# Reciprocal square roots on VectorE, residual steps scheduled earlier, three up-projection steps interlaced

## The chip, the core and the metric

The kernel runs on one core of one Trainium2 chip. The metric is the device time of one execution in microseconds. The core's engines run at the same time, each through its own queue in order: TensorE (PE in the profile, its weight loads PEld), VectorE (DVE), ScalarE (ACT), GpSimd (POOL) and SyncE (SP), which issues the weight loads.

## What is computed

A decoder trunk of four layers over one sequence of 256 tokens, 1024 wide, in float32. Each layer is a token mixer and a squared-ReLU MLP, each behind an RMS norm and added to the residual; the mixers are differential attention (layers 0 and 3), block-sparse MoBA (layer 1) and sliding-window attention with sinks (layer 2). A last RMS norm ends it.

```python
def rms_norm(x, g):
    y = x * rsqrt(mean(x * x, axis=-1, keepdims=True) + 1e-6)
    return y * g

def diff_attention(h, ...):                 # layers 0 and 3, 8 heads
    ...
    p = softmax(s)                          # two score maps for each head
    p = p[:, :, 0] - lam * p[:, :, 1]
    o = einsum('bhqk,bkhe->bqhe', p, v)
    o = rms_norm(o, sub_g) * (1.0 - lambda_init)
    return o.reshape(B, S, H * 128) @ w_out

def sqrelu_mlp(h, w_up, w_down):
    a = maximum(h @ w_up, 0)
    return (a * a) @ w_down

for i in range(4):
    h = h + mixer[i % 3](rms_norm(h, attn_norm_g[i]))
    h = h + sqrelu_mlp(rms_norm(h, mlp_norm_g[i]), w_up[i], w_down[i])
return rms_norm(h, final_norm_g)
```

So there are reciprocal square roots of three kinds: one for each layer's first norm, one for each head in the two differential layers, and one for the final norm. (The second norm of each layer goes through the squared ReLU: its factor is applied afterwards as a plain reciprocal of the mean square.)

## The kernel before

**Weights.** All weights come as pieces of 128 x 2048 float32 (1 MB). `fetch` issues the load of one piece on SyncE's queue into one of four `raw` buffers. `stage` splits it into a high part `whi` (ScalarE, line 80) and the remainder `wlo` (VectorE, line 81), in two halves of 1024 columns. `take` hands out a piece, having fetched five and staged two ahead. Activations are split in the same way, and each product is three matmuls: high by high, high by low, low by high. `mm3` (lines 267 to 269) writes three of 256 columns for the output projections; `block_step` (lines 605 and following) does it with two matmuls, one 512 columns wide over both halves of the activation (`hi`) and one 256 wide (`lo`).

**Layout.** The residual is kept transposed in four tiles `hT`, each with two of the eight 128-row blocks d. `into` (lines 615 to 628) adds a finished block of a projection to `hT` (VectorE, line 625) and calls `norm_part`, which makes that block's part of the next norm's input: `hg`, the residual times the gain, its high part on ScalarE (line 224) and its low part on VectorE (line 225). `norm_sum` gathers the squares.

**First norm of a layer.** The input projection `p_in` (line 292) runs on `hg` without the norm's factor. `norm_factor` sums the squares with a matmul (`p_sum`), makes `nx` (VectorE, line 247) and takes the root: `nr`, by `rsqrt` (lines 206 and 207). The first readers of `nr` apply it to the output of `p_in`: ScalarE in layers 0, 1 and 3 (`qk`, line 589), VectorE in layer 2 (`rest`, line 495, then rope, lines 300 to 305, then the transposes `p_qk`, line 461).

**Differential heads.** In layers 0 and 3 heads go in pairs, four pairs a layer. `diff_pair` multiplies by the values (`p_av`), sums squares on ScalarE (`junk`), makes `ss` (VectorE, line 399), the root `ry`, the scaled output `o` (VectorE, line 403, which reads the PSUM bank of `p_av`), its transposes `p_o` (line 408) and their split `oo`. New heads' queries and keys go through `p_qk`, `qhl`, `kpadh` (ScalarE, line 477) and `kpadl` (VectorE, line 478), the scores through `p_s` and the readings `ns` (line 332).

**Output projection.** `out_proj_all` (layers 0, 2, 3) holds all eight blocks in four PSUM banks (`p_d`) and goes through four pieces; `rest()` finishes the last heads within it. Only the fourth piece (g = 3) completes a block, and `into` follows for each of the eight. Layer 1 uses `out_proj`.

**MLP.** `up_proj` takes 16 pieces; each gives two blocks of 128 hidden rows in two banks (`p_up`), over eight input blocks k. For the first piece (g = 0) the steps are sorted by k, so that TensorE can begin when the first `hg` is there; then for k = 0 to 7 comes a step for b = 0 and one for b = 1. `down_proj` follows.

**Order.** The program is written as straight code; a scheduler places the instructions of each engine by priority, which by default is the order in the code, and by its own estimate of when the inputs are there. So one engine's queue is fixed when the program is built, and an edit can move instructions far from it. PSUM is used as two groups of four banks, "wk" (scores, transposes, `p_up`) and "acc" (`p_in`, `p_d`).

Of the kernel before, what the change touches and what calls it, by code (L numbers as in the profile page):

```python
# [11 lines left out]
F32 = mybir.dt.float32  # L12
F32R = mybir.dt.float32r
I32 = mybir.dt.int32
AF = mybir.ActivationFunctionType
OP = mybir.AluOpType
AX = mybir.AxisListType

P = 128
D = 1024  # L20
S = 256
NT = S // P
# [12 lines left out]
def f(ap):  # L35
    return ap.bitcast(F32)
# [3 lines left out]
def trunk(ctx: ExitStack, tc: tile.TileContext, xT, gains, lams, swa_row, fng, weights, out):  # L40
    nc = tc.nc
    V, A, G, T = nc.vector, nc.scalar, nc.gpsimd, nc.tensor

    cst = ctx.enter_context(tc.tile_pool(name="cst", bufs=1))
    tiny = ctx.enter_context(tc.tile_pool(name="tiny", bufs=2))
# [3 lines left out]
    def bank(tag, name):  # L49
        return ps.tile([P, 512], F32, tag=tag, name=name, bufs=4)  # L50
# [44 lines left out]
    def r3(n):  # L95
        return lambda t: t.rearrange("p (a b) -> p a b", a=n)
# [29 lines left out]
    invt = cst.tile([P, NT, 8], F32, name="invt")  # L126
    for j in range(8):
        G.memset(invt[:, :, j:j + 1], float(inv[j]))
    minus_half = cst.tile([P, 2 * NT], F32, name="minus_half")
    G.memset(minus_half, -0.5)  # L130
    make_identity(nc, ident)

# [70 lines left out]
            V.tensor_scalar(nlam[:, s:s + 1], nlam[:, s:s + 1], -lam_init[s], None, op0=OP.add)  # L203
            V.tensor_scalar(sg[:, s:s + 1], sg[:, s:s + 1], 1.0 - lam_init[s], None, op0=OP.mult)

    def rsqrt(y, x):
        G.tensor_tensor(y, x, minus_half[:, :x.shape[-1]], op=OP.pow)


    class Normed:  # L210
# [30 lines left out]
    def mean_square(n):  # L241

        p = bank("wk", "p_sum")
        for t in range(NT):
            T.matmul(p[:, P * t:P * t + P], n.acc[:, P * t:P * t + P], ones, start=True, stop=True)
        x = tiny.tile([P, NT], F32, tag="nx", name="nx", bufs=8)
        V.tensor_scalar(x, p[:, :S].rearrange("p (t m) -> p t m", m=P)[:, :, 0], 1.0 / D, EPS, op0=OP.mult, op1=OP.add)
        return x

    def norm_factor(n):  # L250

        x = mean_square(n)
        r = tiny.tile([P, NT], F32, tag="nr", name="nr")
        rsqrt(r, x)
        return r

    def mean_row(n):
# [96 lines left out]
    def times_v(o, et, v):  # L354

        T.matmul(o(0), et[:, 0:P], v(0), start=True, stop=True)
        T.matmul(o(1), et[:, P:2 * P], v(0), start=True, stop=False)
        T.matmul(o(1), et[:, 2 * P:3 * P], v(1), start=False, stop=True)
# [9 lines left out]
    def part(b, n=1):  # L368

        if b % 2 == 0:  # L370
            pair[:] = [room(14 + b // 2, [P, 2, 2, S], "oo", F32R)]
        return pair[0] if n == 2 else pair[0][:, b % 2]
# [17 lines left out]
    def diff_pair(slot, ets, v, el, b):  # L390

        p = bank("wk", "p_av")
        for c in range(2):
            times_v(lambda t, c=c: p[:, S * c + P * t:S * c + P * t + P], ets[c], v[c])
        ss = tiny.tile([P, 2 * NT], F32, tag="ss", name="ss")
        for t in range(2 * NT):
            junk = sb.tile([P, P], F32, tag="junk", name="junk", bufs=1)
            A.activation(junk, p[:, P * t:P * t + P], AF.Square, accum_out=ss[:, t:t + 1])
        V.scalar_tensor_tensor(ss, ss, 1.0 / P, el, op0=OP.mult, op1=OP.add)
        y = tiny.tile([P, 2 * NT], F32, tag="ry", name="ry")  # L400
        rsqrt(y, ss)
        o = sb.tile([P, 2 * NT, P], F32, tag="o", name="o")
        V.tensor_tensor(o, p.rearrange("p (t m) -> p t m", m=P), y[:, :, None].to_broadcast([P, 2 * NT, P]),
                        op=OP.mult)
        yield
        p = bank("wk", "p_o")
        for t in range(2 * NT):
            T.transpose(p[:, P * t:P * t + P], o[:, t, :], ident)
        both, gain = part(b, 2), sg[:, slot:slot + 1]
        A.activation(both[:, :, 0], r3(2)(p), AF.Copy, scale=gain)  # L410
        V.scalar_tensor_tensor(both[:, :, 1], r3(2)(p), gain, f(both[:, :, 0]), op0=OP.mult, op1=OP.subtract)
        yield [both[:, 0], both[:, 1]]
# [66 lines left out]

    def mixer_layer(i, n):  # L480
        mixer, slot = i % 3, i // 3
        r = norm_factor(n)
        parts = []
        kpad = new_keys()
        if mixer == 2:
# [6 lines left out]
            p = proj(n, (256, 1), True)  # L492
            kv = rest[:, 512:1024].rearrange("p (t c) -> p t c", t=NT)
            for t in range(NT):
                V.scalar_tensor_tensor(kv[:, t, :], p[t], r[:, t:t + 1], rest[:, :256],
                                       op0=OP.mult, op1=OP.add)
# [4 lines left out]
            for c in range(4):  # L501
                p = proj(n, (256, 1), False, first)
                qn = room(c % 2, [P, NT, 256], "qn")
                for t in range(NT):
                    for h in range(2):
                        s = slice(P * h, P * h + P)
                        o = qn[:, t, :].rearrange("p (b h e) -> p b h e", h=2, e=HD)[:, :, h, :]
# [19 lines left out]
        else:  # L527
# [40 lines left out]
            order = (0, 1, "v", 2, 3, "v") if mixer else (0, 1, "v", 2, "v", 3)  # L568
# [9 lines left out]
            for at, c in enumerate(order):  # L578
                p = proj(n, (512, 2), at == 0, [lambda do=do, x=x: do(x) for do, x in plan[2 * at]])
# [22 lines left out]

    def block_step(p, hi, lo, x, start, stop):
        T.matmul(r3(2)(p), hi, x, start=start, stop=False, skip_group_check=True)  # L606
        T.matmul(p[:, :S], lo, x[:, 0], start=False, stop=stop, skip_group_check=True)  # L607

    def joined(out, p):

        cross = sb.tile([P, S], F32, tag="cross", name="cross")
        A.activation(cross, p[:, S:], AF.Copy)  # L612
        V.tensor_tensor(out, p[:, :S], cross, op=OP.add)  # L613

    def into(n, d, p, row, whole=False):

        j, b = d // 2, d % 2
        h = hT[j][:, S * b:S * b + S]
        y = p
        if not whole:  # L620
            y = sb.tile([P, S], F32, tag="y", name="y")
            joined(y, p)
        if row is not None:
            V.tensor_tensor(y, y, row, op=OP.mult)
        V.tensor_tensor(h, y, h, op=OP.add)  # L625
        norm_part(n, d)
        if b:
            norm_sum(n, j)

    def out_proj_all(parts, n, rest):  # L630

        banks = [bank("acc", f"p_d{j}") for j in range(4)]
        for g in range(4):
            hi, lo = (r3(2)(x) for x in take())
            for d in range(8):
                if (g, d) == (2, 4):
                    rest()
                p = banks[d // 2][:, S * (d % 2):S * (d % 2) + S]
                w = slice(P * d, P * d + P)
                for a in range(2):  # L640
                    x = parts[2 * g + a]
                    mm3(p, hi[:, a, w], lo[:, a, w], x[:, 0], x[:, 1], g + a + d % 2 == 0, g + a == 4,
                        skip_group_check=True)
                if g == 3:
                    into(n, d, p, None, True)

    def out_proj(parts, n, rest):

# [16 lines left out]
    def up_proj(n, then):  # L665

        us = []
        for g in range(16):
            hi, lo = (r3(8)(x) for x in take())
            ps_up = [bank("wk", "p_up") for _ in range(2)]  # L670
            order = [(b, k) for b in range(2) for k in range(8)]
            for b, k in order if g else sorted(order, key=lambda x: x[1]):
                w = slice(P * b, P * b + P)
                block_step(ps_up[b], hi[:, k, w], lo[:, k, w], n.both[k // 2][:, k % 2], k == 0, k == 7)
            t = sb.tile([P, 512], F32, tag="relu", name="relu")
            for b in range(2):
                joined(t[:, S * b:S * b + S], ps_up[b])
            u = sb.tile([P, 512], F32, tag="u", name="u")
            V.scalar_tensor_tensor(u, t, 0.0, t, op0=OP.max, op1=OP.mult)  # L679
            both = room(g, [P, 2, 2, S], "uu", F32R)  # L680
            A.activation(both[:, :, 0], r3(2)(u), AF.Copy)  # L681
            V.tensor_tensor(both[:, :, 1], r3(2)(u), f(both[:, :, 0]), op=OP.subtract)  # L682
            us += [both[:, b] for b in range(2)]
            then(g)
        return us
# [10 lines left out]
    def down_out(us, res, factor):  # L696
# [3 lines left out]
        ss = cst.tile([P, 4, NT], F32, name="fss")  # L700
        x = cst.tile([P, 2, NT], F32, name="fx")
        r = cst.tile([P, NT], F32, name="fr")
# [10 lines left out]
        def finish(t, halves):  # L713

            o = slice(t, t + 1)
            y = r[:, o]
            V.scalar_tensor_tensor(x[:, 1, o], ss[:, halves, o], 1.0 / D, x[:, 0, o], op0=OP.mult, op1=OP.add)
            rsqrt(y, x[:, 1, o])
            rows = slice(P * t, P * t + P)
            A.activation(res[t][:, :512], res[t][:, :512], AF.Copy, scale=y)  # L720
            nc.scalar.dma_start(out[rows, :512], res[t][:, :512])
            for z in (slice(512, 768), slice(768, 1024)):
                V.scalar_tensor_tensor(res[t][:, z], res[t][:, z], y, grow[:, z], op0=OP.mult, op1=OP.mult)
                nc.sync.dma_start(out[rows, z], res[t][:, z])
# [7 lines left out]
        for c in range(2):  # L732
# [22 lines left out]
            if c == 0:  # L755
                last(1, ends)
                close(1, banks[1], 0, 0)
                for t in range(NT):
                    y = res[t][:, :512]
                    V.tensor_tensor(y, y, grow[:, :512], op=OP.mult)  # L760
                    sofar(t, [])
            else:
# [4 lines left out]
                for h in range(2):  # L767
                    p = bank("acc", "p_last")[:, :256]
# [8 lines left out]
    n = new_norm(gv[:, 0, 0, :])  # L777
# [5 lines left out]
    for i in range(DEPTH):  # L783
        parts, rest = mixer_layer(i, n)
        n = new_norm(gv[:, 1, i, :])
# [24 lines left out]
        if i + 1 < DEPTH:  # L810
            n = new_norm(gv[:, 0, i + 1, :])
# [81 lines left out]
```

## Time and profile before

| | |
|---|---|
| median of 3 runs | 1145.63 us (1145.61 to 1146.57) |
| the profiled execution, its own time | 1146.1 us |
| its span | 1144.3 us (1.8 us lie around it) |
| granted TensorE clock, mean | 0.998 |
| powers on GpSimd (line 207) | 14 in 14.5 us: ry 8, nr 4, fr 2 |
| tensor work: weights read | 196.52 MB, 173 GB/s over the span |

The profile is of one execution. A line of a group gives line, engine, operation, output and inputs, the count, then busy time and mean duration in ns of one instruction, then the idle time of the engine just before these and what ended it. The chain of waits is followed back from the last instruction; its columns are start, length and what ran. The timeline lists instructions by start and length. "POOL" is GpSimd, "DVE" VectorE, "ACT" ScalarE.

### The profile page before, as it was taken

How to read it: one execution, taken by the hardware profiler on the slowest of the kernel's cores; microseconds unless marked ns; L12 is line 12 of the kernel's file. 1: busy time of each engine (PE TensorE's matmuls, PEld its weight loads, DVE VectorE, ACT ScalarE, POOL GpSimd, SP SyncE). 2: the span in 40 equal slices, each digit the busy share in tenths (PEclk: the TensorE clock that was granted, in tenths of full speed). 3: DMA queues.
4: the chain of work that ended last, by engine and by line, in shares of the span. 5: the costliest groups of instructions: out<-in, count | busy, mean ns of one | idle time of the engine just before them, and what ended most of it. 6: DMA issues, size and time to landing. Idle time of an engine off the chain costs nothing.

```text
span 1144.3 us, 16938 instructions
## 1 busy us (share of the span) xinstructions
PE 1135.1 (99%) x6560; PEld 987.1 (86%) x6560; DVE 808.9 (71%) x1474; ACT 660.6 (58%) x1207; POOL 25.9 (2%) x54
## 2 busy tenths in 40 slices
PE   9999999999999999999999999999999999999997
PEld 7889888888888888888899898888888889888886
DVE  7867977656576698776568887775657677777453
ACT  7866655544476665654446866554447666665332
POOL 2000000000100000000010000000010000000000
PEclk9999999999999999999999999999999999999999
DMA  8543455555544355555563346555553434555551
GB/s 327 199 147 118 167 198 189 198 198 184 184 143 151 115 182 190 198 200 185 184 208 111 111 148 220 184 185 187 185 201 130 148 143 153 188 198 180 184 184 37
DMA packets 30608, 198.66 MB, mean 174 GB/s; under 512 B 3520, under 2 KB 5184, under 8 KB 7360
## 3 DMA queue, kind: packets, MB, share of 16 engines
q1 hardware_dynamic: 30240, 197.06, 49.6%
q8 instruction: 51, 0.84, 0.3%
q10 hardware_dynamic: 288, 0.52, 0.1%
q14 instruction: 29, 0.24, 0.1%
HBM read 196.52 MB, written 1.05 MB: 173 GB/s over the span
## 4 chain that ended last, share of the span: by engine, by line
PE 94%; DVE 2%; issue 1%; ACT 1%; DMA 0%; POOL 0%; SPq 0%; POOLq 0%; DVEq 0%; ACTq 0%
PE p_up L606 21%; PE p_in L292 18%; PE p_down L606 15%; PE p_up L607 11%; PE p_down L607 8%; PE p_last L269 2%; PE p_last L268 2%; PE p_last L267 2%; PE p_d L268 2%; PE p_d L269 2%; PE p_d L267 2%; PE p_t L350 1%; DVE wlo L81 1%; PE p_s L267 1%; PE p_s L268 1%; PE p_av L432 1%
## 5 line engine op out<-in xcount | busy, mean ns | idle before, releaser
L81 DVE TENSOR_TENSOR wlo<-raw,whi 128x1024 fp32r<-128x1024 f32 (+1 forms) x374 | 446.8, 1210 | 210.6 <-ACT whi L80 210.1
L80 ACT ACTIVATE whi<-raw 128x1024 fp32r<-128x1024 f32 (+1 forms) x374 | 384.4, 1046 | 208.7 <-issue 107.0
L606 PE MATMUL p_up<-hg,whi 128*128 128x512 f32 x1024 | 356.7, 393 | 0.6 <-DVE hg L225 0.4
L607 PE MATMUL p_up<-hg,wlo 128*128 128x256 f32 x1024 | 284.8, 279 | 0.0
L606 PE MATMUL p_down<-uu,whi 128*128 128x512 f32 x768 | 266.4, 392 | 0.0
L606 PEld LDWEIGHTS p_up<-hg,whi 128*128 128x128 f32 x1024 | 191.5, 187 | 43.4 <-PE p_d L269 0.8
L607 PE MATMUL p_down<-uu,wlo 128*128 128x256 f32 x768 | 214.3, 279 | 0.0
L292 PE MATMUL p_in<-whi,hg 128*128 128x512 f32 (+1 forms) x736 | 212.3, 372 | 0.0
L607 PEld LDWEIGHTS p_up<-hg,wlo 128*128 128x128 f32 x1024 | 193.2, 189 | 0.5
L606 PEld LDWEIGHTS p_down<-uu,whi 128*128 128x128 f32 x768 | 143.7, 187 | 32.1
L292 PEld LDWEIGHTS p_in<-whi,hg 128*128 128x128 f32 x736 | 132.5, 189 | 23.4 <-ACT hg L224 0.4
L607 PEld LDWEIGHTS p_down<-uu,wlo 128*128 128x128 f32 x768 | 144.8, 189 | 0.0
L292 PE MATMUL p_in<-wlo,hg 128*128 128x512 f32 (+1 forms) x368 | 130.3, 368 | 0.2
L681 ACT ACTIVATE uu<-u 128x512 fp32r<-128x512 f32 x64 | 40.5, 633 | 70.7 <-DVE u L679 70.7
L292 PEld LDWEIGHTS p_in<-wlo,hg 128*128 128x128 f32 x368 | 68.9, 189 | 11.9 <-DVE wlo L81 1.0
L612 ACT ACTIVATE cross<-p_up 128x256 f32<-128x256 f32 x128 | 48.2, 376 | 39.3 <-PE p_up L607 33.8
L224 ACT ACTIVATE hg<-hT,gn 128x256 fp32r<-128x256 f32 x64 | 31.6, 503 | 65.5 <-DVE hT L625 65.2
L335 ACT ACTIVATE e<-ns,nm 128x128 f32<-128x128 f32 (+1 forms) x128 | 56.7, 446 | 14.3 <-DVE nm L332 14.2
L682 DVE TENSOR_TENSOR uu<-u,uu 128x512 fp32r<-128x512 f32 x64 | 44.2, 691 | 21.2 <-ACT uu L681 21.2
L267 PE MATMUL p_d<-oo,whi 128*128 128x256 f32 x192 | 55.1, 287 | 0.0
L268 PE MATMUL p_d<-oo,whi 128*128 128x256 f32 x192 | 55.1, 287 | 0.0
L613 DVE TENSOR_TENSOR relu<-p_up,cross 128x256 f32<-128x256 f32 x128 | 53.6, 419 | 1.6 <-ACT cross L612 1.2
(175 smaller groups left out, 1239.3 us busy)
## 6 DMA issues: line engine op xcount, KB each, us to landing
raw<-in_weights SPq DMA_DIRECT2D x181, 1024.0 KB, 4.8
raw<-in_weights SPq DMA_DIRECT2D x8, 256.0 KB, 4.9
raw<-in_weights SPq DMA_DIRECT2D x4, 512.0 KB, 7.1
hT<-in_xT SPq DMA_DIRECT2D x8, 128.0 KB, 4.8
bias<-in_swa_row SPq DMA_DIRECT2D x1, 512.0 KB, 3.7
grow<-in_fng SPq DMA_DIRECT2D x1, 512.0 KB, 3.6
out<-res SPq DMA_DIRECT2D x4, 128.0 KB, 2.1
out<-res ACTq DMA_DIRECT2D x2, 256.0 KB, 2.2
```

Source lines behind the costliest of these rows:

```text
L80: A.activation(hi[:, s], raw[:, s], AF.Copy)
L81: V.tensor_tensor(lo[:, s], raw[:, s], f(hi[:, s]), op=OP.subtract)
L267: T.matmul(out, lh, rh, start=start, stop=False, **kw)
L268: T.matmul(out, lh, rl, start=False, stop=False, **kw)
L269: T.matmul(out, ll, rh, start=False, stop=stop, **kw)
L292: T.matmul(out[t], n.both[k // 2][:, k % 2, x, P * t:P * t + P], r3(kb)(parts[k // kb][w])[:, k % kb, :], start=fresh, stop=k == 7 and x + ...
L335: A.activation(e[:, s], ns[:, s], AF.Exp, bias=nm[:, t:t + 1], scale=-1.0, accum_out=l[:, t:t + 1])
L606: T.matmul(r3(2)(p), hi, x, start=start, stop=False, skip_group_check=True)
L607: T.matmul(p[:, :S], lo, x[:, 0], start=False, stop=stop, skip_group_check=True)
L612: A.activation(cross, p[:, S:], AF.Copy)
L613: V.tensor_tensor(out, p[:, :S], cross, op=OP.add)
L682: V.tensor_tensor(both[:, :, 1], r3(2)(u), f(both[:, :, 0]), op=OP.subtract)
```

## The change

Three edits.

1. `rsqrt` gets a length and a switch. With `by_power` it is the power on GpSimd as before; this is kept in the first norm of layer 0 and in the final norm. Elsewhere (the other three `nr`, all eight `ry`) it is ten VectorE instructions: one on the integer view of the number gives a first guess, and three rounds of Newton's iteration of three instructions each refine it. The scratch tile `nw` has seven buffers; `nx` goes from eight buffers to one, and the constant of minus one half is as wide as the remaining powers need.
2. In `out_proj_all` the call of `into` after the fourth piece stands under a high priority, so the scheduler places its steps (`hT`, `hg` on both engines, the squares) ahead of other work that is ready.
3. In `up_proj`, for the first piece, the eighth, ninth and tenth steps are no longer wide, narrow, wide, narrow, wide, narrow but wide 8, wide 9, narrow 8, wide 10, narrow 9, narrow 10. `block_step` gets an argument that says which of its two matmuls it issues.

The number of matmuls, of ScalarE instructions and of loads is the same; VectorE has 110 instructions more, GpSimd 11 fewer.

```diff
@@ -126,7 +126,7 @@
     invt = cst.tile([P, NT, 8], F32, name="invt")
     for j in range(8):
         G.memset(invt[:, :, j:j + 1], float(inv[j]))
-    minus_half = cst.tile([P, 2 * NT], F32, name="minus_half")
+    minus_half = cst.tile([P, NT], F32, name="minus_half")
     G.memset(minus_half, -0.5)
     make_identity(nc, ident)
 
@@ -203,8 +203,17 @@
             V.tensor_scalar(nlam[:, s:s + 1], nlam[:, s:s + 1], -lam_init[s], None, op0=OP.add)
             V.tensor_scalar(sg[:, s:s + 1], sg[:, s:s + 1], 1.0 - lam_init[s], None, op0=OP.mult)
 
-    def rsqrt(y, x):
-        G.tensor_tensor(y, x, minus_half[:, :x.shape[-1]], op=OP.pow)
+    def rsqrt(y, x, n, by_power=False):
+
+        if by_power:
+            G.tensor_tensor(y, x, minus_half[:, :n], op=OP.pow)
+            return
+        t = tiny.tile([P, n], F32, tag="nw", name="nw", bufs=7)
+        V.tensor_scalar(y.bitcast(I32), x.bitcast(I32), -0.5, 1597463007.0, op0=OP.mult, op1=OP.add)
+        for _ in range(3):
+            V.tensor_tensor(t, y, y, op=OP.mult)
+            V.scalar_tensor_tensor(t, t, -0.5, x, op0=OP.mult, op1=OP.mult)
+            V.scalar_tensor_tensor(y, t, 1.5, y, op0=OP.add, op1=OP.mult)
 
 
     class Normed:
@@ -243,15 +252,15 @@
         p = bank("wk", "p_sum")
         for t in range(NT):
             T.matmul(p[:, P * t:P * t + P], n.acc[:, P * t:P * t + P], ones, start=True, stop=True)
-        x = tiny.tile([P, NT], F32, tag="nx", name="nx", bufs=8)
+        x = tiny.tile([P, NT], F32, tag="nx", name="nx", bufs=1)
         V.tensor_scalar(x, p[:, :S].rearrange("p (t m) -> p t m", m=P)[:, :, 0], 1.0 / D, EPS, op0=OP.mult, op1=OP.add)
         return x
 
-    def norm_factor(n):
+    def norm_factor(n, by_power):
 
         x = mean_square(n)
         r = tiny.tile([P, NT], F32, tag="nr", name="nr")
-        rsqrt(r, x)
+        rsqrt(r, x, NT, by_power)
         return r
 
     def mean_row(n):
@@ -398,7 +407,7 @@
             A.activation(junk, p[:, P * t:P * t + P], AF.Square, accum_out=ss[:, t:t + 1])
         V.scalar_tensor_tensor(ss, ss, 1.0 / P, el, op0=OP.mult, op1=OP.add)
         y = tiny.tile([P, 2 * NT], F32, tag="ry", name="ry")
-        rsqrt(y, ss)
+        rsqrt(y, ss, 2 * NT)
         o = sb.tile([P, 2 * NT, P], F32, tag="o", name="o")
         V.tensor_tensor(o, p.rearrange("p (t m) -> p t m", m=P), y[:, :, None].to_broadcast([P, 2 * NT, P]),
                         op=OP.mult)
@@ -479,7 +488,7 @@
 
     def mixer_layer(i, n):
         mixer, slot = i % 3, i // 3
-        r = norm_factor(n)
+        r = norm_factor(n, i == 0)
         parts = []
         kpad = new_keys()
         if mixer == 2:
@@ -602,9 +611,11 @@
 
 
 
-    def block_step(p, hi, lo, x, start, stop):
-        T.matmul(r3(2)(p), hi, x, start=start, stop=False, skip_group_check=True)
-        T.matmul(p[:, :S], lo, x[:, 0], start=False, stop=stop, skip_group_check=True)
+    def block_step(p, hi, lo, x, start, stop, which="hl"):
+        if "h" in which:
+            T.matmul(r3(2)(p), hi, x, start=start, stop=False, skip_group_check=True)
+        if "l" in which:
+            T.matmul(p[:, :S], lo, x[:, 0], start=False, stop=stop, skip_group_check=True)
 
     def joined(out, p):
 
@@ -642,7 +653,8 @@
                     mm3(p, hi[:, a, w], lo[:, a, w], x[:, 0], x[:, 1], g + a + d % 2 == 0, g + a == 4,
                         skip_group_check=True)
                 if g == 3:
-                    into(n, d, p, None, True)
+                    with tc.high_priority():
+                        into(n, d, p, None, True)
 
     def out_proj(parts, n, rest):
 
@@ -669,9 +681,19 @@
             hi, lo = (r3(8)(x) for x in take())
             ps_up = [bank("wk", "p_up") for _ in range(2)]
             order = [(b, k) for b in range(2) for k in range(8)]
-            for b, k in order if g else sorted(order, key=lambda x: x[1]):
+            if g == 0:
+                order.sort(key=lambda x: x[1])
+
+            def up(b, k, which):
                 w = slice(P * b, P * b + P)
-                block_step(ps_up[b], hi[:, k, w], lo[:, k, w], n.both[k // 2][:, k % 2], k == 0, k == 7)
+                block_step(ps_up[b], hi[:, k, w], lo[:, k, w], n.both[k // 2][:, k % 2], k == 0, k == 7, which)
+
+            steps = [(x, "hl") for x in order]
+            if g == 0:
+
+                steps[7:10] = [(order[7 + x], w) for x, w in ((0, "h"), (1, "h"), (0, "l"), (2, "h"), (1, "l"), (2, "l"))]
+            for (b, k), which in steps:
+                up(b, k, which)
             t = sb.tile([P, 512], F32, tag="relu", name="relu")
             for b in range(2):
                 joined(t[:, S * b:S * b + S], ps_up[b])
@@ -715,7 +737,7 @@
             o = slice(t, t + 1)
             y = r[:, o]
             V.scalar_tensor_tensor(x[:, 1, o], ss[:, halves, o], 1.0 / D, x[:, 0, o], op0=OP.mult, op1=OP.add)
-            rsqrt(y, x[:, 1, o])
+            rsqrt(y, x[:, 1, o], 1, True)
             rows = slice(P * t, P * t + P)
             A.activation(res[t][:, :512], res[t][:, :512], AF.Copy, scale=y)
             nc.scalar.dma_start(out[rows, :512], res[t][:, :512])
```

## The prediction

> **What bounds the kernel now.** I read the page's totals first, then who waits for what on TensorE, then the chain that ended last, and only at the gaps the timeline. The row of digits below is VectorE's busy share, in tenths, of 40 slices of 28.6 us.
>
> ```profile
> span 1144.3 us, 16938 instructions
> PE 1135.1 (99%) x6560; PEld 987.1 (86%) x6560; DVE 808.9 (71%) x1474; ACT 660.6 (58%) x1207; POOL 25.9 (2%) x54
> DVE  7867977656576698776568887775657677777453
> PE 94%; DVE 2%; issue 1%; ACT 1%; DMA 0%; POOL 0%; SPq 0%; POOLq 0%; DVEq 0%; ACTq 0%
> ```
>
> TensorE sets the end almost everywhere: 94% of the chain. The change adds no matmul and takes none away, so it can earn only what TensorE loses between matmuls. Waits that TensorE's own records show are few:
>
> ```profile
> PE p_qk L461 <- DVE rest L305: 0.6, 1, 0.6
> PE p_up L606 <- DVE hg L225: 0.4, 2, 0.2
> ```
>
> Ends of matmuls are modelled and overlap the next one, so a wait shorter than the pipeline does not appear there. I therefore take the distance between starts. The chain shows where to look:
>
> ```profile
> 96.57 0.38 PE p_s L267
> ...
> 116.41 2.35 DVE wlo L81 x2
> 118.76 0.41 DVE hg L225
> 119.30 0.47 PE p_up L606
> ...
> 599.51 1.55 POOL nr L207
> 601.08 0.89 DVE rest L495 x2
> 602.73 0.44 PE p_qk L461 x2
> ...
> 662.88 2.35 DVE wlo L81 x2
> ...
> 932.80 1.02 POOL ry L207
> ...
> 954.44 2.35 DVE wlo L81 x2
> ```
>
> Three kinds of place: the last head of a differential mixer (layers 0 and 3, near 96 and 934), where a power stands in the chain or beside it; the start of the up projection (119, 666, 957), where a gain step (hg) stands behind two weight splits (2.35 us); and the start of layer 2 (602), behind a power of 1.54 us. The change touches each.
>
> **Part 1: the root moves from GpSimd to VectorE.** Eight powers ry and three of the four nr go. Their prices:
>
> ```profile
> L207 POOL TENSOR_TENSOR ry<-ss,minus_half 128x4 f32<-128x4 f32 x8 | 8.1, 1008 | 172.5 <-DVE ss L399 141.2 <-DVE el L385 31.3
> L207 POOL TENSOR_TENSOR nr<-nx,minus_half 128x2 f32<-128x2 f32 x4 | 5.3, 1334 | 41.7 <-DVE nx L247 28.5 <-DVE an L180 13.2
> ```
>
> In their place stand ten VectorE instructions each, 110 in all: one on the integer view of the number, then three times a product and two scalar_tensor_tensor. The nearest rows (and ss below, 0.15 to 0.16), and two instructions of which the second needs the first:
>
> ```profile
> L247 DVE TENSOR_SCALAR nx<-p_sum 128x2 f32<-128x2 f32 x5 | 0.8, 152 | 0.0
> L157 DVE CAST posf<-gn 128x2 f32<-128x2 int32 x1 | 0.5, 537 | 1.6 <-DMA gn<-in_gains 1.6
> ```
>
> ```profile
> 17.26 0.17 DVE L177 TENSOR_TENSOR turns<-an,an_lo 128x16 f32<-128x16 f32 x1
> 17.46 0.18 DVE L178 TENSOR_TENSOR an<-an,turns 128x16 f32<-128x16 f32 x1
> ```
>
> A dependent instruction starts about 0.03 us after the one before ends (17.26 + 0.17 = 17.43, next start 17.46). Ten of 0.155 with 0.034 between them: a root of 1.9 us. The integer step has no like in the trace. Bounds: 0.15 us, as nx, and 0.54 us, as the one row that reads int32. I take 0.15, because it is a tensor_scalar on 128x4 and not a cast; the other end adds 0.4 us to each root.
>
> The power's path, from ss to o:
>
> ```profile
> 64.30 0.16 DVE L399 SCALAR_TENSOR_TENSOR ss<-ss,el 128x4 f32<-128x4 f32 x1
> 65.59 0.69 DVE L403 TENSOR_TENSOR o<-p_av,ry 128x512 f32<-128x512 f32 x1 [1.13 <-POOL ry L207]
> 67.72 0.60 PE L408 MATMUL p_o<-ident,o 128*128 128x128 f32 x4
> ```
>
> From ss's end (64.46) to o is 1.13 us; with the root it is 1.9. So o is 0.8 us later, ends near 67.1, and the transposes p_o stand at 67.72: 0.6 us to spare, cost nothing, covered by eight p_qk ahead of them. If that cover were gone it would be 0.8 us a pair. The second and the fourth pair have more. VectorE has room: 6 and 7 tenths busy in the slices from 57 to 114, so over 17 us free of 57, while four roots add 7.6.
>
> The third pair stands in the gap:
>
> ```profile
> 94.49 0.15 DVE L399 SCALAR_TENSOR_TENSOR ss<-ss,el 128x4 f32<-128x4 f32 x1
> 95.58 0.28 PE L269 MATMUL p_d<-oo,wlo 128*128 128x256 f32 x1
> 95.82 0.69 DVE L403 TENSOR_TENSOR o<-p_av,ry 128x512 f32<-128x512 f32 x1 [0.59 <-POOL ry L207]
> 95.91 1.04 PE L267 MATMUL p_s<-kpadh,qhl 128*128 128x256 f32 x3
> 96.55 0.69 DVE L478 TENSOR_TENSOR kpadl<-p_qk,kpadh 64x512 fp32r<-64x512 f32 x1
> 97.03 0.28 PE L269 MATMUL p_d<-oo,wlo 128*128 128x256 f32 x1
> 97.30 0.39 PE L268 MATMUL p_s<-kpadl,qhl 128*128 128x256 f32 x1
> 99.03 0.60 PE L408 MATMUL p_o<-ident,o 128*128 128x128 f32 x4
> ```
>
> One 256-column matmul of the output projection follows another after 0.12 us, a 512-column one takes 0.23. Against that the first p_s starts 0.21 late (95.58 to 95.91 is 0.33), the third 0.21 late (it takes the bank that o reads, and o ends at 96.51; it starts at 96.57), and the next, on the second kpadl, 0.15 (97.03 to 97.30 is 0.27). Together 0.57; the second p_s row of the chain, 96.57, is that third one. In the changed program the p_s takes a bank that p_qk frees, the second kpadl stands on VectorE ahead of the remaining root steps, and five more p_d (0.6 us) come before the first p_s. o moves to an end near 98.9, and p_o, 0.5 earlier than 99.03 but behind those five p_d, stands at 99.1: 0.1 to 0.2 us to spare, the thinnest cover of the whole change. I take 0.5 of the 0.57, and the same in layer 3: **minus 1.0**.
>
> Layer 2's start:
>
> ```profile
> 599.21 0.15 DVE L247 TENSOR_SCALAR nx<-p_sum 128x2 f32<-128x2 f32 x1
> 599.28 1.22 DVE L81 TENSOR_TENSOR wlo<-raw,whi 128x1024 fp32r<-128x1024 f32 x1
> 601.84 0.28 PE L292 MATMUL p_in<-wlo,hg 128*128 128x256 f32 x1
> ```
>
> TensorE loses 602.73 - 601.84 - 0.12 = 0.77. The power runs beside a split (599.28 to 600.50). In the changed program the same split stands on VectorE before the root, so the root runs from 600.5 to 602.4, and the chain behind it (601.08 to 602.73, 1.6 us) ends near 604.1: 1.4 later. But the changed TensorE order has 18 more p_in ahead of p_qk, 18 x 0.12 = 2.16, which puts p_qk at 601.96 + 2.16 = 604.12. What is left is 0.1 to 0.2 us of the 0.77 lost: **minus 0.58**. Without that cover it would be plus 1.5. The later p_qk there (qn) have 0.4 us to spare. Layers 1 and 3 cost nothing: VectorE stands idle there for longer than a root,
>
> ```profile
> 312.13 1.23 DVE L81 TENSOR_TENSOR wlo<-raw,whi 128x1024 fp32r<-128x1024 f32 x1 [3.26 <-ACT whi L80]
> ```
>
> and the first reader is ScalarE at 312. Layer 0's first norm and the final one keep the power.
>
> [...]
>
> **Part 2: residual steps ahead of splits.** The changed order on VectorE puts hT and the first hg between or before the wlo that stood ahead of them.
>
> ```profile
> 118.81 0.28 PE L269 MATMUL p_d<-oo,wlo 128*128 128x256 f32 x1
> 119.61 0.28 PE L607 MATMUL p_up<-hg,wlo 128*128 128x256 f32 x1
> ```
>
> In layer 0 TensorE loses 119.30 - 118.81 - 0.12 = 0.37, and 119.61 - 119.30 - 0.23 = 0.08 behind the first p_up. The first hg stood behind two splits of 2.35 us together; in the changed order only half of one is between, which makes it ready near 118.7. The first p_up moreover comes behind 12 more p_d (they used to come after it), near 119.8, so 1 us is to spare. The chain has the same 2.35 us of splits before hg in layers 2 and 3; I take the same there, three times 0.45, rounded down: **minus 1.3**. The splits that are passed are late next, by two steps of 0.42 and two of 0.48 us at most; the up projection's first piece is already split by then, and the matmuls of one piece (16 x (0.23 + 0.12) = 5.6 us) cover it. If they did not, the 1.3 would come back. No DMA is issued by the steps moved; the loads on SP's queue stand in the same order and wait for buffers that the splits free.
>
> **Part 3: three steps interlaced.** The same 16 wide and 16 narrow matmuls, three pairs in another order. The trace has no such order; bounds: 0.2 us a layer either way (one narrow matmul's 0.12 and a little). I take 0.
>
> **Sum**: 1.0 + 0.58 + 1.3 = 2.88. The profiled execution took 1146.1 (1144.3 and 1.8 around it), so it would become 1143.2; it is 0.5 above the median of the runs, 1145.63, which would become **1142.8**. The term not worked out is the reordered rest of layer 2: 0.5 either way.
>
> **Rivals.** (a) The root is dear: the integer step costs 0.54. The third pair's o then ends past p_o's place by 0.2 to 0.3 in two layers, and layer 2's rest is 0.4 later: 0.9 less, 1143.7. For it: the only int32 row. Against: it is a cast. (b) The head starts are given back: TensorE reaches the next fixed thing earlier, such as the split of the next piece, and waits there. Then 1.3 and half of the tails go, 1144.5. For it: VectorE is nearly full just there (9 tenths or more in the slice from 114 to 143). Against: the chain of waits names no split in that stretch after the first p_up, so the supply keeps up. (c) Slower: VectorE takes its instructions in order, and a root is ten that depend on each other; what stands behind them on the queue (kpadl, the readings of p_s, the next split) comes 0.8 us later in each of eight pairs. It decides when the root passes 2.1 us in the third pair or 2.5 in the first, or when the 18 p_in of layer 2 wait themselves for a split. If half of the pairs pay (4 x 0.8) and layer 2 pays 1.5, against 1.3 gained: plus 3.4, 1149.0; all eight: 1152.2. For it: covers of 0.1 to 0.6. Against: the free time of VectorE above. (d) The priority moves nothing: 1.3 less gain, 1144.1; against it stands the changed order itself, so 0.02.
>
> [...]
>
> **How the numbers follow.** Chances: the forecast 0.58, (a) 0.14, (b) 0.11, (c) 0.15, (d) 0.02. What a measurement of this kernel can tell from no change is about 0.2%, 2.29 us: the border is at 1143.34 and 1147.92. The forecast's own range is 1141.8 to 1143.9 (0.5 for layer 2's rest, 0.8 for part 3, the spare 0.2 of the tails); 0.49 of its 0.58 lies below the border. (a), (b) and (d) lie inside, with 0.02 of (c). Faster 0.49, same 0.38, slower 0.13. The range leaves out most of (c) and holds the rest: 1141.0 to 1146.6.
>
> **What would show it.** Right: p_up in layers 0, 2 and 3 starts 0.12 us after the last p_d; no wait of TensorE on hg in the waits view; the gap before layer 2's first p_qk under 0.3; ten small VectorE steps taking 1.9 us from ss to o; GpSimd without ry. Wrong: an integer step near 0.5 us; p_o of the third pair waiting for o; gaps in the up projection's second piece; TensorE waiting for wlo among layer 2's first p_in.

## The result, and the profile after

The changed kernel takes 1143.18 us (median of 11 runs, 1142.86 to 1144.43) against 1145.83 of before (11 runs, 1145.48 to 1146.63). The ratio is 0.9978, with a 95% interval of 0.9969 to 0.9988: 2.65 us less, between 1.4 and 3.6. Its profiled execution has a span of 1141.1 us, where before had 1144.3.

From the page after, the row of engines and the chain by engine; from the waits, what is left of TensorE's:

```profile
PE 1132.7 (99%) x6560; PEld 983.2 (86%) x6560; DVE 824.5 (72%) x1584; ACT 661.2 (58%) x1207; POOL 13.2 (1%) x43
PE 97%; DVE 1%; issue 1%; ACT 1%; DMA 0%; SPq 0%; POOL 0%; POOLq 0%; DVEq 0%
```

```profile
PE p_warm L135 <- POOL ones L124: 1.0, 1, 1.0
```

The same 6560 matmuls; VectorE has 15.6 us more work and GpSimd half of its own; TensorE's share of the chain went from 94% to 97%, and both waits shown before (rest, hg) are gone. Only the warm-up's wait at the very start remains.

The new root, in the groups by line (duration in ns behind the comma):

```profile
L214 DVE TENSOR_TENSOR nw<-ry 128x4 f32<-128x4 f32 x24 | 3.9, 162 | 0.8
L216 DVE SCALAR_TENSOR_TENSOR ry<-nw,ry 128x4 f32<-128x4 f32 x24 | 3.9, 162 | 0.7
L215 DVE SCALAR_TENSOR_TENSOR nw<-nw,ss 128x4 f32<-128x4 f32 x24 | 3.9, 161 | 0.7
L212 DVE TENSOR_SCALAR ry<-ss 128x4 int32<-128x4 int32 x8 | 1.3, 159 | 0.1
```

and at layer 2's start, in the timeline of VectorE and TensorE:

```profile
597.81 1.22 DVE L81 TENSOR_TENSOR wlo<-raw,whi 128x1024 fp32r<-128x1024 f32 x1
598.94 0.16 DVE L212 TENSOR_SCALAR nr<-nx 128x2 int32<-128x2 int32 x1
600.70 0.16 DVE L216 SCALAR_TENSOR_TENSOR nr<-nw,nr 128x2 f32<-128x2 f32 x1
600.90 0.88 DVE L504 SCALAR_TENSOR_TENSOR rest<-p_in,nr,rest 128x256 f32<-128x256 f32 x2
602.53 0.28 PE L301 MATMUL p_in<-wlo,hg 128*128 128x256 f32 x1
602.82 0.44 PE L470 MATMUL p_qk<-ident,rest 128*128 128x128 f32 x2
```

The integer step takes 159 ns like its neighbours; a root takes 1.92 us (598.94 to 600.86). The split still stands ahead of it, and the gap before p_qk is 0.29 - 0.12 = 0.17 us, where it was 0.77.

The last head of layer 0 and the start of its up projection, same views:

```profile
95.07 0.28 PE L278 MATMUL p_d<-oo,wlo 128*128 128x256 f32 x1
95.37 0.61 PE L276 MATMUL p_s<-kpadh,qhl 128*128 128x256 f32 x2
96.18 0.28 PE L276 MATMUL p_d<-oo,whi 128*128 128x256 f32 x1
96.33 0.38 PE L277 MATMUL p_s<-kpadl,qhl 128*128 128x256 f32 x1
97.81 0.68 DVE L412 TENSOR_TENSOR o<-p_av,ry 128x512 f32<-128x512 f32 x1
98.87 0.60 PE L417 MATMUL p_o<-ident,o 128*128 128x128 f32 x4
...
119.26 0.28 PE L278 MATMUL p_d<-oo,wlo 128*128 128x256 f32 x1
119.38 0.40 PE L616 MATMUL p_up<-hg,whi 128*128 128x512 f32 x1
```

The p_s that waited for o's bank now goes straight on; the first still starts 0.18 late. o ends at 98.49, 0.38 ahead of p_o. The first p_up starts 0.12 after the last p_d: no gap.

All records of TensorE are there in every trace of this study, so the n-th matmul of a name in one trace can be set against the n-th in another. The table, worked out from those starts (one trace of each kernel), gives for each stretch how much shorter (-) or longer (+) than before it became, in us. "Tail" runs from the 28th (114th) p_qk to the 16th (32nd) p_o; "up" of layers 0 and 2 from the last p_o or the 400th p_d to the next p_row; "first piece" of layer 3 from the last p_o to the last p_res; "rest of up" from there to the first p_last; "whole" from the 28th p_qk to the last p_last, with the stretches that have no column of their own. The first stretch of the kernel, to the 28th p_qk, is left out: it moved by -0.62 to +1.17 between these executions.

| kernel | tail 0 | up 0 | MLP 0 to layer 2's p_sum | layer 2 mixer | up 2 | tail 3 | first piece 3 | rest of up 3 | whole |
|---|---|---|---|---|---|---|---|---|---|
| changed | -0.47 | -0.47 | 0.00 | -0.77 | -0.44 | -0.47 | -0.48 | 0.00 | -3.19 |
| roots only | -0.45 | -0.02 | +0.10 | -0.77 | 0.00 | -0.48 | -0.03 | 0.00 | -1.67 |
| priority only | 0.00 | -0.33 | 0.00 | -0.03 | -0.28 | 0.00 | -0.34 | +1.48 | +0.55 |
| interlacing only | 0.00 | +0.01 | +3.69 | -0.03 | -0.02 | -0.02 | -0.03 | 0.00 | +3.62 |
| roots and priority | -0.47 | -0.33 | +0.06 | -0.78 | -0.28 | -0.48 | -0.33 | +1.48 | -1.10 |

Behind the last p_last something is lost that the table does not have. From that matmul's start to the end of the span, before takes 6.59 us and the changed kernel 7.06. The difference stands among GpSimd's closing instructions: the last drain there begins 0.36 us after the instruction ahead of it, in place of 0.03, and takes 0.18 us in place of 0.03. All eight kernels here in which all eleven roots stand on VectorE have it (7.06 to 7.09 us), the six others, before among them, do not (6.5 to 6.6); the cause is not known. So of the 3.19 us that TensorE wins, some 2.7 are left at the end, which is what the runs show (2.65).

### The profile page after: what moved, and what is told of

Read it like the earlier page. It is cut to its first block, busy times and chain, and to the rows that moved or that the text cites. A ratio compares the mean times of both kernels' runs of the same rounds, so it can differ in the third digit from the quotient of the medians.

```text
span 1141.1 us, 17026 instructions
## 1 busy us (share of the span) xinstructions
PE 1132.7 (99%) x6560; PEld 983.2 (86%) x6560; DVE 824.5 (72%) x1584; ACT 661.2 (58%) x1207; POOL 13.2 (1%) x43
## 4 chain that ended last, share of the span: by engine, by line
PE 97%; DVE 1%; issue 1%; ACT 1%; DMA 0%; SPq 0%; POOL 0%; POOLq 0%; DVEq 0%
PE p_up L616 21%; PE p_in L301 19%; PE p_down L616 16%; PE p_up L618 10%; PE p_down L618 8%; PE p_last L278 2%; PE p_last L277 2%; PE p_last L276 2%; PE p_d L276 2%; PE p_d L278 2%; PE p_d L277 2%; PE p_t L359 1%; PE p_s L276 1%; PE p_qk L470 1%; PE p_av L441 1%; PE p_s L277 1%
## 5 line engine op out<-in xcount | busy, mean ns | idle before, releaser
L278 PE MATMUL p_d<-oo,wlo 128*128 128x256 f32 x192 | 54.2, 286 | 0.0
```

The costliest lines, as they stand in the source:

```text
L278: T.matmul(out, ll, rh, start=False, stop=stop, **kw)
```

## The experiments

Each kernel was measured beside runs of before, whose medians in these sessions lay between 1145.90 and 1146.18 us; the ratios are against these. The intervals reach about 0.1%, over 1 us, to either side, so most of the terms below are told apart by the starts of the traces and not by the times.

### Each edit alone, and the change without the interlacing

Roots only: `into` without the priority and

```diff
-                steps[7:10] = [(order[7 + x], w) for x, w in ((0, "h"), (1, "h"), (0, "l"), (2, "h"), (1, "l"), (2, "l"))]
+                pass
```

> Roots on VectorE alone; no priority, no interlacing. My theory (each edit closes its own gaps): TensorE gains 0.47 in the last head of layer 0, 0.47 in that of layer 3 and 0.6 to 0.8 around layer 2's start, and still loses 0.37 to 0.45 before the first p_up of layers 0, 2 and 3. Together 1.6 to 1.8 us less than before, some 1144.1. Rival (the order under the priority earns all of it, and a root that is 0.8 us longer costs): no gain in the last heads, time 1145.8 or above. Rival (VectorE's strict order makes roots costly): 1147 or more.

Measured: 1144.74 us (11 runs), ratio 0.9988 (0.9979 to 0.9997). The theory's stretches are there to a tenth: both tails and layer 2. That is 1.67 of the changed kernel's 3.19 us.

Priority only: before with

```diff
-                    into(n, d, p, None, True)
+                    with tc.high_priority():
+                        into(n, d, p, None, True)
```

> Priority alone; all roots by power, no interlacing. My theory: 0.37 to 0.48 gained before the first p_up of layers 0, 2 and 3, about 1.3 to 1.4 us, some 1144.4; the gaps in the last heads (0.57 of p_s) and the 0.77 before layer 2's first p_qk stay as before. Rival (the order earns all): some 1142.9, the last heads' gaps are closed as well.

Measured: 1146.58 us, ratio 1.0005 (0.9996 to 1.0014); 1144.4 was expected. The gaps before p_up closed (0.37, 0.28 and 0.37 us in before), but the first pieces won only 0.3 each, and 1.48 us were lost in layer 3's up projection, where nothing was edited and no wait stands. How many matmuls began or ran in the same 60 us there (the windows; behind PE busy stands the count), in this kernel and then in the changed one:

```profile
974.00:1034.00 60.00, 60.00 (x341) 51.99 (x341) 44.57 (x63) 34.43 (x53) 0.00 (x0) 1.00 0.53 180
```

```profile
974.00:1034.00 60.00, 60.00 (x348) 52.44 (x347) 45.75 (x63) 35.64 (x54) 0.00 (x0) 1.00 0.57 193
```

TensorE is busy without a break in both, at a granted clock of 1.00, and gets 341 matmuls through against 348. Its pace is another.

Interlacing only: the changed kernel with all roots by power and without the priority.

> Interlacing alone; all roots by power, no priority. My theory: TensorE's starts after the up projection's first piece stand as before within 0.1 us in each layer; time 1145.8 within 0.5. Rival (the interlaced order hides or exposes a wait on a late hg): each layer's first piece gets 0.1 to 0.3 shorter or longer, up to 1.2 us in all.

Measured: 1149.29 us (median of 7; five runs lie at 1149.28 to 1149.61, the others at 1145.47 and 1146.59), ratio 1.0020 (1.0009 to 1.0030). Neither theory. The whole loss lies in one stretch, layer 1's MLP with the output projection ahead of it, and again as pace (510 to 570 us, in this kernel, then in before):

```profile
510.00:570.00 60.00, 60.00 (x341) 52.04 (x340) 34.55 (x43) 26.52 (x34) 0.00 (x0) 1.00 0.54 188
```

```profile
510.00:570.00 60.00, 60.00 (x348) 52.47 (x347) 33.49 (x43) 26.36 (x35) 0.00 (x0) 1.00 0.55 190
```

It is there from 388.6 us on, in layer 1's output projection and ahead of the layer's interlaced piece, so that piece did not start it; nor did it end it. By their times two of the seven runs of this same program went without the loss; only one with it was traced.

Roots and priority, no interlacing (the `pass` above):

> Roots and priority, without interlacing. My theory: the sum of the two, 3.0 to 3.2 us less than before in TensorE's starts, the time of the changed kernel within 0.4 us (1143.2). Rival (the interlacing is what lets the early hg pay): 0.3 to 1.2 slower than the changed kernel.

Measured: 1145.37 us, ratio 0.9994 (0.9985 to 1.0003). The rival held, though for more than its 1.2 us: without the interlacing 2.2 us are missing. By the table, 0.14 to 0.16 in each first piece and 1.48 in layer 3.

### Two paces

A wide matmul has 512 columns, a narrow one 256. In layer 3 of the changed kernel both paces stand next to each other (timeline of TensorE, wide matmuls of the first piece; "x2" are the neighbours that the interlacing made):

```profile
956.97 0.40 PE L616 MATMUL p_up<-hg,whi 128*128 128x512 f32 x1
957.32 0.40 PE L616 MATMUL p_up<-hg,whi 128*128 128x512 f32 x1
957.68 0.40 PE L616 MATMUL p_up<-hg,whi 128*128 128x512 f32 x1
958.03 0.40 PE L616 MATMUL p_up<-hg,whi 128*128 128x512 f32 x1
...
958.38 0.64 PE L616 MATMUL p_up<-hg,whi 128*128 128x512 f32 x2
...
959.79 0.39 PE L616 MATMUL p_up<-hg,whi 128*128 128x512 f32 x1
960.13 0.40 PE L616 MATMUL p_up<-hg,whi 128*128 128x512 f32 x1
960.48 0.39 PE L616 MATMUL p_up<-hg,whi 128*128 128x512 f32 x1
960.82 0.40 PE L616 MATMUL p_up<-hg,whi 128*128 128x512 f32 x1
```

Three wide-narrow pairs take 1.06 us ahead of the x2 and 1.03 to 1.04 behind it. In the exact starts the slow cycle is 233, 117, 241, 120, 236, 113 ns (wide, narrow, and so on: 1060 for three pairs, 353.3 a pair), the fast ones 346.7 a pair (230 and 117, or 232, 118, 230, 113 and the like). 6.7 ns a pair is 1.9%: small in a piece, 1.48 us in the rest of an up projection.

So the theory became: after a run of p_d the pairs fall into the slow cycle and stay in it until something breaks it. In before the late hg did that unasked: the scheduler had put a narrow matmul and two wides out of turn where the first piece meets the second, and the slow cycle ended there (in layer 0 at 127.2 us, 4.8 us after it began). With the priority hg is early, nothing is out of turn, and the cycle lasts. Two runs tell in which layer the interlacing counts:

```diff
-            if g == 0:
+            if g == 0 and len(ups) == 4:
```

> The changed kernel with the interlacing in layer 3's first piece alone. Theory of two cycles (after a run of narrow matmuls the wide-narrow pairs of the up projection fall into a cycle of 353.3 ns a pair, in place of 346.7, and stay in it until something breaks it; two wides next to each other break it): the slow cycle stands from the first p_up to p_row in layers 0 and 2, 0.15 us lost in each against the changed kernel, and layer 3's up projection is fast (the 1.48 us of the run without interlacing are not lost). Time 1143.5. Rival (each layer's interlacing is worth the same, about 0.5 us): 1144.9.

Measured: 1143.68 us, ratio 0.9981 (0.9972 to 0.9991); the rest of layer 3's up projection is fast, layers 0 and 2 lose 0.14 and 0.16.

With `len(ups) < 4` instead:

> The changed kernel with the interlacing in layers 0 to 2 only. Theory of two cycles: layer 3's up projection runs at 353.3 ns a pair from its first piece to its last, 1.5 to 1.65 us lost against the changed kernel, time 1144.8; layers 0 and 2 as in the changed kernel. Rival (each layer's interlacing is worth the same): 1143.7.

Measured: 1145.08 us, ratio 0.9992 (0.9983 to 1.0002); +1.48 in layer 3, and a slow stretch from layer 1's output projection on (0.40), which its interlaced piece did not end; it ended in the piece behind, at 417.1 us. The layers do not count alike, and layer 3 is as the theory has it; that two wides did not end the cycle in layer 1 is against it.

A smaller disturbance:

```diff
-((0, "h"), (1, "h"), (0, "l"), (2, "h"), (1, "l"), (2, "l"))
+((0, "h"), (1, "h"), (0, "l"), (1, "l"), (2, "h"), (2, "l"))
```

> The changed kernel with the smaller disturbance wide 8, wide 9, narrow 8, narrow 9 and step 10 untouched. Theory of two cycles, with any two neighbouring wides as what breaks it: as the changed kernel, 346.7 ns a pair from there on, 1143.2. Rival (the exact order of the six matters): the slow cycle stays, 2.0 us more, 1145.2.

Measured: 1143.65 us, ratio 0.9979 (0.9969 to 0.9988). Layers 0, 2 and 3 are as in the changed kernel within 0.02; 0.5 is lost to a slow stretch in layer 1, which these two wides did not end.

That left the rule "any two neighbouring wides". It was tested far from a stage's start, with `if g == 8 and len(ups) == 4`:

> Roots and priority; the interlacing moved out of the first pieces, to the ninth piece (g = 8) of layer 3's up projection alone. Theory of two cycles: layer 3's up projection runs at 353.3 ns a pair until the ninth piece, some 45 us after its start, and at 346.7 from the very place of the six reordered matmuls on; 0.6 of the 1.48 us are lost there, and 0.15 more in each first piece of layers 0, 2 and 3. Time 1144.5. Rival (the slow cycle belongs to the stage, by its data or its traffic, and the interlacing acts only where the stage begins): 353.3 to the end, 1145.4.

Measured: 1145.50 us, ratio 0.9994 (0.9985 to 1.0003): the rival's number, and layer 3 keeps its full +1.47. Timeline of TensorE there, wide matmuls:

```profile
1006.72 0.40 PE L616 MATMUL p_up<-hg,whi 128*128 128x512 f32 x1
...
1007.78 0.63 PE L616 MATMUL p_up<-hg,whi 128*128 128x512 f32 x2
...
1008.83 0.40 PE L616 MATMUL p_up<-hg,whi 128*128 128x512 f32 x1
...
1009.89 0.40 PE L616 MATMUL p_up<-hg,whi 128*128 128x512 f32 x1
```

1.06 us for three pairs ahead of the x2, 1.06 behind: the cycle was disturbed and came back. My rule fell; that the stage's data or traffic holds the cycle, as the rival says, is not shown by it. One thing that differs is the place in the cycle. Neighbouring wides met the slow cycle with the one of 241 ns as the first of the two 27 times (layers 0, 2 and 3; in before and in the roots-only run by the scheduler's own order), and it ended there each time; in interlaced pieces with the one of 236 seven times (layer 1 of four runs, and the other layers of the interlacing-only run, where it ended 3 us later at the scheduler's own two wides), and it did not end there; with the one of 233 once, here, and it did not. So with hg early the eighth step is the right one, and in layer 1, or with hg late, it is not.

The place is not all of it. In every kernel the scheduler itself puts two wides next to each other at the start of layer 1's second piece. Four traces met them in the slow cycle, and it ended in one (interlacing in layers 0 to 2), where the first of the two stands in the place of the 233. It stayed in three: in two (interlacing only, priority and interlacing) from that same place, and in one (two wides) from the place of the 241. In two more (roots only, interlacing in layer 3 alone) the pairs were fast ahead of them and slow for 4 us behind. All this is a reading of traces; moving the x2 by a step in the ninth piece was not tried.

Priority and interlacing without the roots:

> Priority and interlacing; all fourteen roots by the power. Theory of two cycles: the priority's gaps before p_up stay closed (0.3 in each of layers 0, 2 and 3) and the slow cycle is broken in every first piece, so 1.4 us less than before, 1144.5, where the priority alone gave 1146.6. Rival (the priority earns nothing without the roots): 1145.9 or more.

Measured: 1149.43 us (9 runs, 1145.98 to 1149.87), ratio 1.0023 (1.0014 to 1.0033). By the number that is the rival's side, not by its reason: the first pieces won 0.46 to 0.49 each, as the theory has it. But layer 1's MLP was slow (+3.60), and layer 3 fell back into the slow cycle behind p_res (+1.49) though its first piece had left it. So a fast first piece does not guarantee the rest: here the slow cycle began again behind an interruption (p_sum and p_res).

### The roots

Powers for the eight ry again:

```diff
-        rsqrt(y, ss, 2 * NT)
+        rsqrt(y, ss, 2 * NT, True)
```

> The changed kernel with the eight ry by the power on GpSimd again; the three nr stay on VectorE. My theory (the tails' 0.47 each come from the root's leaving the path of o and of the bank it reads): the gaps of p_s in the last heads of layers 0 and 3 are back, 0.9 to 1.0 more, 1144.1; layer 2's start keeps its 0.77. Rival (the tails' gain comes from the order, not from the root's engine): 1143.2, no gaps.

Measured: 1143.78 us, ratio 0.9982 (0.9972 to 0.9991); both tails are at 0.00 against before, and the other stretches of the table as in the changed kernel. The time rose by 0.60 us and not by the 0.94 of the tails; the stretch behind the last p_last, 6.59 us here, takes 0.47 of them back. The timeline shows the wait that returned (power, o, and TensorE's weight load that waits for o's bank):

```profile
94.16 1.01 POOL L209 TENSOR_TENSOR ry<-ss,minus_half 128x4 f32<-128x4 f32 x1 [12.54 <-DVE ss L408]
95.20 0.69 DVE L412 TENSOR_TENSOR o<-p_av,ry 128x512 f32<-128x512 f32 x1 [0.59 <-POOL ry L209]
95.94 0.19 PEld L276 LDWEIGHTS p_s<-kpadh,qhl 128*128 128x128 f32 x1 [0.35 <-DVE o L412]
```

Powers for the three nr again:

```diff
-        rsqrt(r, x, NT, by_power)
+        rsqrt(r, x, NT, True)
```

> The changed kernel with the three nr of layers 1 to 3 by the power again; the eight ry stay on VectorE. My theory: the gap before layer 2's first p_qk is back to 0.7 or so, layers 1 and 3 start as in the changed kernel, the tails keep their gain; 0.6 to 0.8 more, 1143.9. Rival (layer 2's gain came with the order that any edit brings): 1143.2.

Measured: 1144.08 us, ratio 0.9982 (0.9972 to 0.9992); layer 2's mixer is back to -0.03, where the rival had it unchanged, and the wait stands in the timeline:

```profile
602.77 0.44 PE L470 MATMUL p_qk<-ident,rest 128*128 128x128 f32 x2 [0.62 <-DVE rest L314]
```

Five rounds in each root, two more than needed:

```diff
-        for _ in range(3):
+        for _ in range(5):
```

> The changed kernel with five rounds of the iteration in place of three in each of the eleven roots: sixteen instructions, 3.1 us, in place of 1.95 (two rounds more than the kernel needs). My theory (the covers are 0.4 us in the tails, 0.6 at the first pairs and about nothing at layer 2's start): o reaches p_o late by 0.8 in each tail, by up to 0.6 in each first pair, and layer 2's first p_qk by 1.0, unless the scheduler puts other matmuls ahead; 1.0 to 3.8 more, 1144.2 to 1147.0. Rival (VectorE has room everywhere, the scheduler hides any root): 1143.2 within 0.4.

Measured: 1159.20 us (4 runs), ratio 1.0115 (1.0100 to 1.0130): 16 us more than the changed kernel, four times the bound. TensorE waits for o itself (waits view). The two long waits, 2.14 and 2.15 us, are not at the third pairs, where I had the thinnest cover, but at the fourth: in layer 0 this pair's ss had come to stand on VectorE behind two splits that waited 4.03 us for their whi, and began at 113.62, where in the changed kernel it begins at 106.36, ahead of the next splits. Then TensorE waits for work queued behind o. Chain and windows of layer 0's tail:

```profile
PE p_o L417 <- DVE o L412: 5.5, 4, 2.1
```

```profile
115.58 2.01 ACT whi L80 x2
117.59 2.33 DVE wlo L81 x2
119.92 0.67 DVE oo L420
120.64 0.58 PE p_d L277
```

```profile
115.40:120.60 5.20, 1.62 (x11) 1.01 (x9) 4.91 (x12) 2.69 (x3) 0.00 (x0) 0.97 0.42 176
120.60:124.00 3.40, 3.36 (x17) 3.36 (x18) 1.24 (x3) 0.87 (x2) 0.00 (x0) 0.55 0.90 306
```

The last pair's oo came to stand behind two more splits, TensorE was busy for 1.62 of 5.2 us, and then its granted clock was 0.55 for 3.4 us. The tails cost 4.8 us each against before, and layer 2's mixer, which the change had made 0.77 shorter, became 1.73 longer. In layer 3's tail the granted clock stayed at 0.50 for 6.8 us (963.35 to 970.18); what sets the length of such a stretch no run shows.

## Why the prediction came out right, and where it did not

The time, 1143.18 against 1142.8, and the sum, 3.19 us of TensorE's starts in the trace (2.65 in the runs) against 2.88, came out. The signs that were named for it appeared too: the first p_up 0.12 us after the last p_d, no wait on hg, a gap of 0.17 before layer 2's first p_qk, a root of 1.9 us. The roots' 1.67 us came by the mechanism that the prediction gives. The rest came by luck: a loss that it did not see and a gain that it put at nothing nearly cancel. None of the signs looked at TensorE's pace. It has no term for the 0.47 us behind the last p_last either. By its steps:

- **Tails, minus 1.0**: -0.94, shown by the run with ry on GpSimd, where they are 0.00. The five more p_d stand ahead of p_o as predicted, but not ahead of the first p_s: 33 p_d come before it in both traces, and it still starts 0.18 late. The spare before p_o of the third pair was 0.38, not 0.1 to 0.2; the first pair's o ended at 66.64 with p_o at 67.21, the 0.6 predicted.
- **Root of 1.9 us**: 1.92. The dear integer step, rival (a), fell: 159 ns. The 0.54 us row that bounded it was no price. In before the cast starts at 2.43 beside a GpSimd fill of 0.42; in the changed kernel it starts later and takes less, and ends at the same moment:

```profile
2.43 0.54 DVE L157 CAST posf<-gn 128x2 f32<-128x2 int32 x1 [1.57 <-DMA gn<-in_gains]
2.48 0.42 POOL L139 MEMSET band<- 128x384 f32 x1
```

```profile
2.47 0.42 POOL L139 MEMSET band<- 128x384 f32 x1
2.63 0.33 DVE L157 CAST posf<-gn 128x2 f32<-128x2 int32 x1 [1.77 <-DMA gn<-in_gains]
```

So it is in all 14 traces: the cast starts anywhere from 2.43 to 2.65 and always ends at 2.96 to 2.97, 0.07 behind the fill's end. At 0.54 and at 0.33 us the row ended at the same place beside that fill, so at least 0.2 us of the 0.54 was no work of the cast; what sets the common end no run shows.

- **Layer 2's start, minus 0.58**: -0.77 over the mixer; the gap before p_qk fell by 0.60, the other 0.17 came elsewhere in the reordered mixer. Shown by the run with nr on GpSimd.
- **Up starts, minus 1.3**: -1.39 in the changed kernel, but not by the priority. The step "in layer 0 TensorE loses ... 0.37 ... and ... 0.08", each closed by an earlier hg, is true of the gap and leaves out what the order with the late hg did by the way: in it the slow cycle ended early. The priority alone won 0.95 there and lost 1.48.
- **Part 3, "I take 0"**: the step that failed, though the time came out. The bounds of 0.2 us a layer came from one narrow matmul, on the assumption that 16 wide and 16 narrow matmuls take the same time in any order. Beside roots and priority the interlacing is worth 2.1 us of the 3.19, 1.48 of them in pieces that it does not touch. With this term at 0 and the priority at 1.3, the sum was right because the two errors belong to each other: added to the roots, the priority costs 0.57 us in place of winning 1.3, and the interlacing gives 2.1 in place of nothing.
- **Rival (b)**, head starts given back, did not come: 0.00 in the stretches behind them, layer 0's MLP and layer 3's rest of up. **Rival (c)**, slower through VectorE's order, has its place in the tails and decides somewhere between a root of 1.9 us and one of 3.1; at 3.1 it costs far more than the 0.8 a pair that I priced, because in that program ss and oo stand behind splits. VectorE's free time between 57 and 114 us in before was 16.4 us by the windows view, a little less than the "over 17" read from the digits.

The slow cycle's cause stays open. Shown are its pace, that it outlives p_sum and p_res in some runs and begins there in others, and that beside the priority the six reordered matmuls end it in the first pieces of layers 0, 2 and 3. Why a stretch takes the one or the other, and why the same program does both in layer 1, was not settled. No version here beats the changed kernel.

## What to carry to other kernels

Where one engine is busy 99%, ask for its pace too, not only for its gaps: count matmuls in equal windows and compare the starts of the n-th of a name between two traces. Run each edit of a bundle alone and leave each out once: here one edit alone was slower, another no faster, and the two together, beside the roots, gave half of the change's gain. A row that is long for its kind may be a wait; look at what ends with it before taking it for a price. A forecast that comes out is not yet one whose steps were right.

## What was not expected of the hardware

- TensorE's wide-narrow pairs have a steady cycle of 353.3 ns beside those of 346.7, at a granted clock of 1.00 and with no wait in the records; a stretch of 170 us stayed in it without a break (424.4 to 594.2 us in layer 1 of the interlacing-only run, 3.2 us lost).
- Two wides in a row ended it from one place of the three-pair cycle and mostly not from others: 27 of 27 times at the wide of 241 ns, none of eight in interlaced pieces at those of 233 and 236, one of four at the scheduler's own pairs in layer 1.
- With all eleven roots on VectorE, GpSimd's closing instructions end 0.46 to 0.50 us later behind the last matmul than in before, in eight kernels of eight.
- A dependent small VectorE instruction cost 0.195 us from start to start in layer 2's root (598.94 to 600.70 for nine steps). The power is less regular: 1.01 us for four numbers a partition (ry), 0.71 (layer 0's nr) or 1.54 (layer 2's) for two.
